# Splitting the first load of a between two DMA queues in a fused matmul, gelu, matmul kernel

## The chip, the core and the metric

The kernel runs on one core of one Trainium2 chip. The core has five engines that run beside each other, each through its own list of instructions: TensorE (PE in the profile, with its weight loads as PEld), VectorE (DVE), ScalarE (ACT), GpSimd (POOL) and SyncE (SP). Sixteen DMA engines move data between the chip's main memory and the core's memory of 128 partitions. The metric is the device time of one execution in microseconds (us); less is better. The time before is the median of three runs.

## The reference

```python
m, k, n, p = 1024, 1024, 2048, 1024     # a: m x k, b: k x n, c: n x p, all float32

def reference(a, b, c):
    h = np.matmul(a, b)
    h = 0.5 * h * (1 + np.tanh(np.sqrt(2 / np.pi) * (h + 0.044715 * h ** 3)))
    return np.matmul(h, c).astype(np.float32)
```

Two matrix products with the tanh form of gelu between them.

## The kernel before

The order of instructions on each engine is written out by hand; each engine runs its list from first to last and waits where an operand is not there yet.

The first product needs a transposed, with k on the partitions. So a's rows are cast to bf16 (`ab`), turned by TensorE with an identity matrix into PSUM (`pt`, L145) and copied by VectorE into `aT` (L146). b is needed with k on the partitions as it is, and only cast to bf16 (`b1`, `b2`). The result of a group of matmuls goes through gelu on ScalarE into `hT`, which the second product, with c, reads. The first columns of the first product are plain matmuls (`mm1`, L114); the rest of it and the whole second product go by a scheme of seven products of quarter matrices (`Seven`, L212), with the sums on VectorE and ScalarE. The output is stored by SP.

The stretch that matters here is the start. `a_part(h, q)` is half h of a's rows (512 rows, as four groups of 128) and quarter q of its columns (256), which is 512 KB. SP's queue issues five loads in float32, in this order:

- L75: `a_part(0, 0)` into `sta[:, 0, 0]`, 512 KB;
- L76: the first two k blocks of b's first 512 columns into `stb[:, 0:2]`, 512 KB;
- L77: `a_part(1, 0)` into `sta[:, 1, 0]`, 512 KB;
- L78: `a_part(0, 1)` into `sta[:, 0, 1]`, 512 KB;
- L79: the third k block of b into `stb[:, 2]`, 256 KB.

All other loads are issued by GpSimd, which casts them to bf16 on the way (L86 to L104: the rest of a into `abq`, of b, then c). GpSimd first copies one element of the first load's tile into `gate` (L81), so that its loads come after that landing.

ScalarE begins with one tiny gelu (L82), before which the activation table is loaded; its next work is a cast of b (L108). TensorE first runs matmuls on a constant (`stir`, L125), and then, in this order: the transposes of `a_part(0, 0)`, six matmuls with k blocks 0 and 1, the transposes of `a_part(1, 0)`, five matmuls, the transposes of `a_part(0, 1)`, and so on. VectorE casts all of `sta[:, 0, 0]` in one instruction (L110, by `cast_a(0, 0, nc.vector)`), copies the first transposes, casts a part of b, copies the second transposes, and shares the cast of `sta[:, 1, 0]` with ScalarE.

Of the kernel before, what the change touches and what calls it, by code (L numbers as in the profile page):

```python
# [19 lines left out]
def kernel(ctx, tc, a, b, c, out):  # L20
    nc = tc.nc
# [18 lines left out]
    def slot(tag, shape, dt, name):  # L40
        return big.tile(shape, dt, name=name, tag=tag)
# [24 lines left out]
    sta = slot("x1", [128, 2, 2, 4, 256], F32, "sta")  # L66
    abq = slot("x3", [128, 4, 2, 4, 256], BF16, "abq")

    def a_part(h, q):
        return av[:, 4 * h:4 * h + 4, ds(q * 256, 256)]  # L70

    def b_part(q):
        return bv[:, 2 * q:2 * q + 2, 0:H]

    nc.sync.dma_start(out=sta[:, 0, 0], in_=a_part(0, 0))  # L75
    nc.sync.dma_start(out=stb[:, 0:2], in_=b_part(0))  # L76
    nc.sync.dma_start(out=sta[:, 1, 0], in_=a_part(1, 0))  # L77
    nc.sync.dma_start(out=sta[:, 0, 1], in_=a_part(0, 1))  # L78
# [20 lines left out]
    for n in range(2):  # L99
        for k in range(0, KT, 4):  # L100
            nc.gpsimd.dma_start(out=b2[:, k:k + 4, ts(n, H)],
                                in_=bv[:, k:k + 4, ds(1024 + n * H, H)])
# [385 lines left out]
```

## Time and profile before

| What | us |
|---|---|
| median of three runs | 117.6 (117.41 to 117.97) |
| span of the profiled execution, first to last instruction | 115.7 |
| TensorE busy in it | 111.1 (96%) |
| VectorE busy | 90.0 (78%) |
| ScalarE busy | 51.4 (44%) |
| GpSimd busy | 17.2 (15%) |

For the profiled execution the page gives its span; the time of the runs holds what lies around the span as well. The granted TensorE clock was 1.000 of full speed. The DMA engines are mostly busy in the first 50 us, with loads, and in the last fifth, with stores. The five loads of SP's queue stand in the profile's rows as `sta<-in_a_dram` and `stb<-in_b_dram`; from issue to landing the three into `sta` took 3.6, 6.1 and 7.0 us, and the two into `stb` 5.3 and 7.1 us.

A row of the timeline gives start, duration, engine, line, operation, what it writes and reads, and in brackets how long the engine was idle before it and what ended that. A row "SPq" or a "DMA_DIRECT2D" is the issuing of a transfer, not the transfer. The chain of waits follows the work that ended last back to the start: each piece is what the next one was released by.

### The profile page before, as it was taken

The page shows a single profiled execution, that of the slowest core. Times are in us where ns is not written, and L with a number is a line of the kernel's source. Part 1 is how long each engine was busy: PE and PEld are TensorE (multiplying, and loading weights), DVE is VectorE, ACT ScalarE, POOL GpSimd, SP SyncE. Part 2 cuts the span into 40 slices and gives each one's busy share as a digit, 9 for nine tenths or more (in the row PEclk, how much of TensorE's full clock was granted, in tenths as well). Part 3 has the DMA queues.
Part 4 walks back from the last instruction along what each step waited for, and adds up shares of the span by engine and source line. Part 5 has one row for each costly group of instructions (what it writes and reads, how often), then busy time and mean ns, then how long its engine had stood idle before and what let it go on. Part 6 is the DMA issues. An engine that isn't in the chain of part 4 may idle for free.

```text
span 115.7 us, 1461 instructions
## 1 busy us (share of the span) xinstructions
PE 111.1 (96%) x542; PEld 77.1 (67%) x542; DVE 90.0 (78%) x107; ACT 51.4 (44%) x86; POOL 17.2 (15%) x29
## 2 busy tenths in 40 slices
PE   7989999999999999999999999999999999999980
PEld 6645555546776447888885444688888888888860
DVE  0347748789999998935699999999999986954770
ACT  5053000999259997166698429500124982000000
POOL 2497755223322000000000000000000000000000
PEclk9999999999999999999999999999999999999999
DMA  2999999999999999998000000060000002014993
GB/s 69 295 381 229 200 199 205 204 208 205 206 211 209 212 213 209 212 210 168 8 0 0 6 0 0 38 235 0 0 0 0 0 4 91 1 73 176 370 363 106
DMA packets 13414, 15.94 MB, mean 138 GB/s; under 512 B 736, under 2 KB 9312, under 8 KB 13408
## 3 DMA queue, kind: packets, MB, share of 16 engines
q0 software_dynamic: 8672, 9.31, 47.6%
q1 hardware_dynamic: 4736, 6.56, 15.8%
q8 instruction: 4, 0.07, 0.3%
q14 instruction: 2, 0.02, 0.0%
HBM read 20.97 MB, written 4.19 MB: 218 GB/s over the span
## 4 chain that ended last, share of the span: by engine, by line
PE 90%; DMA 5%; SPq 1%; DVE 1%; issue 0%
PE ps L212 76%; PE ps L114 11%; DMA sta<-in_a_dram 5%; PE pt L145 3%; SPq L76 0%; DVE ab L110 0%; SPq L75 0%; DVE ot L375 0%
## 5 line engine op out<-in xcount | busy, mean ns | idle before, releaser
L212 PE MATMUL ps<-x,s 128*128 128x512 f32 x128 | 29.6, 391 | 0.0
L212 PEld LDWEIGHTS ps<-x,s 128*128 128x128 f32 x128 | 24.0, 188 | 5.1
L212 PE MATMUL ps<-x,x 128*128 128x512 f32 x96 | 22.9, 394 | 0.0
L212 PEld LDWEIGHTS ps<-x,x 128*128 128x128 f32 x96 | 18.0, 188 | 3.9
L114 PE MATMUL ps<-aT,b 128*128 128x512 bf16 x64 | 16.1, 379 | 0.2 <-DVE b L110 0.2
L298 ACT ACTIVATE v<-ps 128x512 f32<-128x512 f32 x10 | 6.0, 599 | 19.1 <-PE ps L212 19.1
L212 PE MATMUL ps<-c_sb,hT 128*128 128x512 bf16 (+1 forms) x72 | 14.2, 356 | 0.0
L212 PE MATMUL ps<-x 128*128 128x512 f32 x56 | 13.2, 392 | 0.0
L212 PEld LDWEIGHTS ps<-x 128*128 128x128 f32 x56 | 10.2, 188 | 2.6 <-ACT u L298 0.4
L118 ACT ACTIVATE hT<-ps 128x512 bf16<-128x512 f32 x14 | 7.3, 595 | 9.7 <-PE ps L114 9.7
L212 PEld LDWEIGHTS <-hT 128*128 128x128 bf16 x72 | 6.9, 98 | 7.0 <-issue 0.5
L118 ACT ACTIVATE hT<-ot 128x512 bf16<-128x512 f32 x18 | 10.4, 624 | 2.0 <-DVE ot L303 2.0
L212 PE MATMUL ps<-aT,b 128*128 128x512 bf16 x48 | 10.7, 379 | 0.0
L146 DVE COPY aT<-pt 128x512 bf16<-128x512 bf16 x16 | 6.7, 423 | 5.1 <-PE pt L145 5.1
L303 DVE TENSOR_TENSOR ot<-ps,u 128x512 f32<-128x512 f32 x10 | 6.7, 690 | 5.1 <-ACT u L298 5.1
L303 DVE TENSOR_TENSOR ot<-ps,v 128x512 f32<-128x512 f32 x10 | 6.7, 688 | 4.8 <-DMA out_dram<-ot 3.8
L170 DVE TENSOR_TENSOR x<-c_sb 128x1024 fp32r<-128x1024 bf16 x8 | 9.3, 1226 | 0.0
L114 PEld LDWEIGHTS <-b 128*128 128x128 bf16 x64 | 5.7, 98 | 4.5 <-DVE b L110 0.3
L212 PEld LDWEIGHTS <-b 128*128 128x128 bf16 x48 | 4.6, 98 | 5.7 <-issue 0.3
L104 POOL DMA_DIRECT2D c_sb<-in_c_dram x8 | 5.6, 702 | 13.1 <-DMA b<-in_b_dram 12.4
L170 DVE TENSOR_TENSOR x<-b 128x1024 fp32r<-128x1024 bf16 (+1 forms) x4 | 7.0, 1752 | 0.6 <-issue 0.6
L298 ACT ACTIVATE u<-ps 128x512 f32<-128x512 f32 x10 | 5.9, 598 | 3.4 <-PE ps L212 3.2
(44 smaller groups left out, 111.3 us busy)
## 6 DMA issues: line engine op xcount, KB each, us to landing
c_sb<-in_c_dram POOLq DMA_DIRECT2D x8, 512.0 KB, 20.0
out_dram<-ot SPq DMA_DIRECT2D x13, 256.0 KB, 2.1
b<-in_b_dram POOLq DMA_DIRECT2D x6, 512.0 KB, 15.3
sta<-in_a_dram SPq DMA_DIRECT2D x3, 512.0 KB, 6.1
abq<-in_a_dram POOLq DMA_DIRECT2D x5, 256.0 KB, 7.9
out_dram<-ot SPq DMA_DIRECT2D x6, 128.0 KB, 2.0
stb<-in_b_dram SPq DMA_DIRECT2D x1, 512.0 KB, 5.3
b<-in_b_dram POOLq DMA_DIRECT2D x2, 256.0 KB, 8.2
```

Of the source, the lines that this page charges most:

```text
L104: nc.gpsimd.dma_start(out=c_sb[:, t:t + 2], in_=cv[:, t:t + 2])
L114: nc.tensor.matmul(p, b1[:, k, ts(t, 128)], aT[:, h, k], start=(k == 0), stop=(k == KT - 1))
L118: nc.scalar.activation(hT[h][:, t], p, AF.Gelu_apprx_tanh)
L145: nc.tensor.transpose(pt[:, n, ts(m, 128)], ab[:, m, ts(n, 128)], ident)
L146: nc.vector.tensor_copy(aT[:, h, 2 * q + n], pt[:, n])
L170: nc.vector.tensor_tensor(out=dst[:, r], in0=x[:, r], in1=y[:, r], op=op)
L212: nc.tensor.matmul(p[:, ds(c0, w)], l[:, k, ts(j, 128)], r[:, k, ds(c0, w)], start=(start and k == 0), stop=(k == self.kt - 1), skip_group ...
L298: nc.scalar.activation(st, p, AF.Copy)
L303: nc.vector.tensor_tensor(out=ot, in0=p, in1=st, op=ADD)
```

## The change

The first of SP's loads is cut in two by groups of rows. The groups 0 and 1 of `a_part(0, 0)` (rows 0 to 255) stay on SP's queue, and the groups 2 and 3 (rows 256 to 511) are issued by ScalarE, ahead of its tiny gelu. Everything else is the same, the instructions that read `sta[:, 0, 0]` included; these now depend on two transfers where they read both parts.

```diff
@@ -72,7 +72,8 @@
     def b_part(q):
         return bv[:, 2 * q:2 * q + 2, 0:H]
 
-    nc.sync.dma_start(out=sta[:, 0, 0], in_=a_part(0, 0))
+    nc.scalar.dma_start(out=sta[:, 0, 0, 2:4], in_=a_part(0, 0)[:, 2:4])
+    nc.sync.dma_start(out=sta[:, 0, 0, 0:2], in_=a_part(0, 0)[:, 0:2])
     nc.sync.dma_start(out=stb[:, 0:2], in_=b_part(0))
     nc.sync.dma_start(out=sta[:, 1, 0], in_=a_part(1, 0))
     nc.sync.dma_start(out=sta[:, 0, 1], in_=a_part(0, 1))
```

## The prediction

> **What bounds the kernel now.** I read the chain that ended last, then that chain in order of time, then the instructions of the first 20 us, then busy time and traffic by stretch. The chain by engine, from the page:
>
> ```profile
> PE 90%; DMA 5%; SPq 1%; DVE 1%; issue 0%
> ```
>
> TensorE is the path for nine tenths of the span; of the rest one load is the largest piece. In order of time (start us, us, what):
>
> ```profile
> 0.74 0.44 SPq L75
> 1.18 0.05 issue
> 1.24 0.50 SPq L76
> ...
> 1.78 6.10 DMA sta<-in_a_dram
> ...
> 7.90 0.44 DVE ab L110
> 8.34 0.05 issue
> 8.38 0.62 PE pt L145 x8
> ...
> 24.46 87.96 PE ps L212 x400
> ```
>
> From 8.38 us on the path is TensorE without a break. What sets 8.38 is the landing, at 1.78 + 6.10 = 7.88 us, of the third load on SP's queue, rows 512 to 1023 of a (L77), not of the load that is changed. So the change can only act through what it does to that landing, through delaying something that has slack now, or outside the span. The instructions around it (start us, us, engine, line, then in brackets the idle time before it):
>
> ```profile
> 0.74 1.28 ACT L82 ACT_TABLE_LOAD   x1 [0.74 <-PEq L472]
> ...
> 4.40 0.69 DVE L110 CAST ab<-sta 128x1024 bf16<-128x1024 f32 x1 [4.40 <-DMA sta<-in_a_dram]
> ...
> 5.08 0.87 POOL L86 DMA_DIRECT2D abq<-in_a_dram  x1
> ...
> 5.58 0.42 DVE L146 COPY aT<-pt 128x512 bf16<-128x512 bf16 x1 [0.49 <-PE pt L145]
> ...
> 6.54 0.94 ACT L108 ACTIVATE b<-stb 128x256 bf16<-128x256 f32 x2 [4.30 <-DMA stb<-in_b_dram]
> 6.54 0.36 DVE L110 CAST b<-stb 128x128 bf16<-128x128 f32 x2 [0.53 <-DMA stb<-in_b_dram]
> ...
> 6.83 1.47 PE L114 MATMUL ps<-aT,b 128*128 128x512 bf16 x6 [0.15 <-DVE b L110]
> ...
> 15.88 0.26 PEld L145 LDWEIGHTS <-abq 128*128 128x128 bf16 x4 [0.28 <-DMA abq<-in_a_dram]
> ```
>
> The first load of a lands just before 4.40. After its cast, transposes and first copy, VectorE stands idle 0.53 us until b lands at 6.54. That 0.53 us is the first load's slack: earlier by itself gains nothing, later by less costs nothing. Then the traffic by stretch (window in us, its length, busy time of each engine, clock, busy share of the DMA engines, and last GB/s):
>
> ```profile
> 1.60:2.00 0.40, 0.40 (x2) 0.31 (x2) 0.00 (x0) 0.40 (x1) 0.00 (x0) 1.00 0.07 26
> 2.00:2.40 0.40, 0.40 (x2) 0.31 (x2) 0.00 (x0) 0.23 (x2) 0.00 (x0) 1.00 0.54 138
> 2.40:2.80 0.40, 0.40 (x3) 0.31 (x2) 0.00 (x0) 0.00 (x0) 0.00 (x0) 1.00 0.91 259
> 2.80:3.60 0.80, 0.80 (x4) 0.62 (x3) 0.00 (x0) 0.00 (x0) 0.00 (x0) 1.00 1.07 364
> ...
> 4.00:5.60 1.60, 1.53 (x10) 1.03 (x9) 0.71 (x2) 0.00 (x0) 1.17 (x2) 1.00 0.91 260
> 5.60:9.00 3.40, 2.92 (x23) 1.66 (x23) 1.71 (x6) 1.56 (x3) 3.40 (x6) 1.00 1.08 380
> ```
>
> All five SP loads are issued by 2.83 + 0.55 = 3.38 us, yet the last lands near 9.93 (2.83 + 7.1 of its tile's view). So the stream is not short of issues: it climbs from nothing to 364 GB/s in one us, sags to 260 in the first b load, and runs at 380 after that.
>
> **The change, part by part.**
> *SP's issue.* One issue of 512 KB becomes one of 256 KB. The five SP issues take 0.44, 0.50, 0.46, 0.51 and 0.55 us, the smallest load the longest, so size does not set them: SP's later issues stay where they are. 0.
>
> *ACT's issue.* One DMA issue, 0.44 to 0.55 us by SP's rows, now ahead of the table load (1.28 us) and the small activation (0.20 us) on ScalarE. Covered by ScalarE's 4.30 us of idleness before 6.54; 0. Without that cover it would be 0.5 us. The same DMA issue is not moved past any SP or POOL issue.
>
> *The stream's start.* The bytes up to the end of L77's load are the same, so L77 lands earlier only if the stream runs better. What the climb loses against 380 GB/s: bytes start at about 1.84 us (finer slices), so 0.16 x 380 - 0.40 x 26 = 50 KB, then 0.40 x (380 - 138) = 97, 0.40 x (380 - 259) = 48, 0.80 x (380 - 364) = 13; together 208 KB, or 208 / 380 = 0.55 us. Two queues that each climb as this one did, added and cut at 380, would have by 2.80 us 20 + 110 + 152 = 282 KB in place of 10 + 55 + 104 = 169, and gain the 13 after it: 126 KB, 0.33 us. If one generator feeds both queues, nothing is gained: 0. If the whole climb went, 0.55. I take 0.3, the two climbs added, since in 2.00 to 2.40 the DMA engines are busy only 0.54 and so have room for a second supply.
>
> *Where the 0.3 us goes.* b, L77, L78 and L79 stand behind it on SP's queue and land as much earlier; VectorE's and ScalarE's casts wait for just these landings. The next thing late would be POOL's stream: TensorE's transposes at 15.93 waited until 15.88 for one of its loads, while TensorE's own work ran to 16.09 on the chain: 0.2 us of slack. POOL's first issue follows the gate copy, which waits for the first load, and POOL's bytes start to move about 9.0 us, as SP's run dry, so the stream should come forward too. If it doesn't, the gain ends at 0.2.
>
> *Second waits.* The first cast waits for two landings (the gate's one element lies in ScalarE's half). By the chain's "issue" pieces a wait costs 0.02 to 0.07 us, inside the 0.53 us of slack: 0.
>
> *Outside the span.* The page gives the span, 115.7 us, alone; the median of the runs is 117.6, so 1.9 us lie around it. ScalarE's hardware queue is not used before; setting it up or closing it is shown by no row. Between 0 and 0.8 us, the longest of SP's closing waits for stores; I take 0, since these waits are for bytes and this queue has been empty for 100 us by then, and keep the 0.8 in the range.
>
> Sum: 117.6 - 0.3 = 117.3 us, a span of 115.4.
>
> One rule speaks against this. The Trainium skill, "DMA: Bandwidth & Descriptors", section "Issuing engines are not separate DMA queues", says that DMAs started by different engines run on the same 16 DMA engines and interleave, and that several issuers save only issue time. By it the sum would be 117.6. This trace shows no second hardware queue at work, so it can neither confirm nor deny it.
>
> **The rivals.**
> *The sag fills too (faster).* If the second queue's reads also overlap the first b load's, part of the stretch 4.00 to 5.60 comes back: 1.60 x (380 - 260) = 192 KB, 0.50 us, on top of 0.3: 116.8. For it: the DMA engines are busy 0.91 at 260 GB/s, so single packets take longer there, as if they waited for memory. Against: ScalarE's half should be in before 4.00, and POOL's slack of 0.2 would then have to move as well.
>
> *ScalarE's half comes late (slower).* Place: ScalarE's queue. If the table load goes first, as it stands first now, the issue comes at 0.74 + 1.28 = 2.02 us and its bytes start 1.1 us later (1.84 - 0.74), at 3.1. SP's half is in by then and b's rows share the engines. 262 KB at a half to a third of some 300 GB/s take 1.75 to 2.6 us, and the last landings came about 0.5 us after the last bytes: the half lands between 5.3 and 6.1. The point from which it decides is 4.40 + 0.53 = 4.93; beyond that VectorE's copy, casts of b and TensorE's first matmuls go back by 0.4 to 1.2 us, and the matmuls stand before the transposes at 8.38. With 0.8: 118.4. For it: the load is ScalarE's first instruction now, at the same 0.74 as SP's first issue. Against: the issue stands ahead of that activation in the program, and the load bears the activation's line.
>
> *ScalarE's queue is starved (slower still).* POOL's first load was issued at 5.08 and no byte of it moved until 9.0, when SP's ran out: the queue view of 4.40 to 9.00 lists SP's queue alone. If ScalarE's half fares so, it lands with SP's last, about 9.9, some 5.5 us late, 5.0 beyond the slack: 122.6. Against: POOL's is a software queue, ScalarE's a hardware one issued together with SP's.
> That wait differs from "Queues, rings and completion order" of the same page of the skill, by which each DMA engine goes round its queues packet by packet; by that rule this rival is worth nothing.
>
> *A closing cost for the second queue:* 117.3 + 0.8 = 118.1. *Nothing at all,* one generator feeding both: 117.6.
>
> **How the numbers follow.** The forecast 0.36, its own range 117.0 to 117.6; the sag filled 0.27; the late half 0.20; starved 0.05; closing cost 0.08; nothing 0.04. A measurement of this kernel tells 0.5%, about 0.6 us, from no change. Faster: 0.27 and 0.04 of the forecast, where all of the climb goes, 0.31. Same: 0.32 of the forecast and 0.04, 0.36. Slower: 0.20 + 0.05 + 0.08 = 0.33. Cases of both signs hold over half, so the range goes from 116.7 (the sag filled, less 0.1 of scatter) to 118.6 (the late half, plus 0.2); starvation and the late half's worst are left out.
>
> **What would show it.** Right: ScalarE's first row an issue near 0.74; more than 138 GB/s in 2.00 to 2.40; the first cast before 4.40; b's casts near 6.2, the cast at 7.90 near 7.6, transposes at 8.1. Wrong: an issue after the table load; a first cast after 4.9; the same climb; a shorter span with the same time around it lost; POOL's stream still starting at 9.0, so that the wait at 15.88 grows.

## The result, and the profile after

The changed kernel takes 117.95 us (median of 22 runs) against 117.56 us before, a ratio of 1.003 with a 95% interval of 1.0019 to 1.0041: slower by 0.39 us by the medians and by 0.35 us by the ratio, where 0.3 us faster was forecast. The profiled execution has a span of 116.5 us against 115.7 us.

The chain of waits of the changed kernel in order of time (start us, us, what), its middle left out:

```profile
0.74 0.44 SPq L76
...
1.75 6.29 DMA sta<-in_a_dram
...
8.54 0.62 PE pt L146 x8
...
24.80 87.98 PE ps L213 x400
112.79 0.02 issue
112.81 0.42 DVE ot L376
```

The same last piece in the chain before:

```profile
112.44 0.42 DVE ot L375
```

The shape of the path is unchanged. Its start came 0.16 us later (8.54 against 8.38), TensorE's long stretch 0.34 us later, and the last addition 0.37 us later. This lateness is within what single executions differ by: six profiles with the changed loads (this one and five of the runs below) have the long stretch begin at 24.41 to 24.94 us, three with the loads as before at 24.46 to 24.81 us. But the span is 0.8 us longer. From the start of the last addition to the end of the span there are 115.67 - 112.44 = 3.23 us before and 116.47 - 112.81 = 3.66 us after (the ends to the hundredth, from the trace): 0.43 us were lost behind the last computation, where the change touches nothing.

Of the start, in the timeline (start us, us, engine, line, idle time before):

```profile
0.74 0.47 ACTq L75 DMA_DIRECT2D sta<-in_a_dram  x1
...
1.24 1.28 ACT L83 ACT_TABLE_LOAD   x1 [1.24 <-PEq L473]
...
4.59 0.69 DVE L111 CAST ab<-sta 128x1024 bf16<-128x1024 f32 x1 [4.59 <-DMA sta<-in_a_dram]
...
6.63 0.36 DVE L111 CAST b<-stb 128x128 bf16<-128x128 f32 x2 [0.35 <-DMA stb<-in_b_dram]
...
16.26 0.23 PEld L146 LDWEIGHTS <-abq 128*128 128x128 bf16 x4 [0.43 <-DMA abq<-in_a_dram]
```

ScalarE issued its half at 0.74 us, as SP did, yet the first load as a whole landed at 4.57 and not 4.38. VectorE's 0.53 us of slack before b's cast shrank to 0.35 us, so this lateness was covered. TensorE's wait for one of GpSimd's loads, 0.28 us before, is 0.43 us in the last row; it put 0.12 us on the path here, but was 0.22 and 0.24 us in two later profiles of the same loads. The traffic by stretch (window, its length, busy times, clock, DMA share, GB/s):

```profile
2.00:2.40 0.40, 0.40 (x2) 0.31 (x2) 0.00 (x0) 0.40 (x1) 0.00 (x0) 1.00 0.82 166
2.40:2.80 0.40, 0.40 (x2) 0.31 (x2) 0.00 (x0) 0.33 (x2) 0.00 (x0) 1.00 0.89 282
2.80:3.60 0.80, 0.80 (x4) 0.62 (x3) 0.00 (x0) 0.00 (x0) 0.00 (x0) 1.00 1.03 316
...
4.00:5.60 1.60, 1.60 (x8) 0.84 (x7) 0.69 (x1) 0.00 (x0) 0.98 (x2) 1.00 0.96 269
```

In 2.00 to 2.80 us this execution has 166 and 282 GB/s, the one before 138 and 259. That is no more than scatter: two later profiles with the loads as before have 146 and 310, and 192 and 323. The sag at 4.00 to 5.60 is still there.

At the end, the view of what SP waited for (engine, line, what: us in total, times, longest) differs. Before:

```profile
SPq L483 <- DMA out_dram<-ot: 1.1, 2, 0.8
```

After:

```profile
SPq L484 <- DMA out_dram<-ot: 1.5, 1, 1.5
```

Before, SP waited for stores twice, at most 0.8 us; after, once, 1.5 us. The trace's rows of SP, from its last store on, show why (ns from the span's start, duration, operation, semaphores; the first of a pair of waits is the completion of a hardware transfer from the second row on). Before, the last store signals semaphore 118:

```
112897 332 DMA_DIRECT2D     semaphore=118
113274  28 EVENT_SEMAPHORE  S[115] S[114]
113344  28 EVENT_SEMAPHORE  S[102] S[113]
113405  28 EVENT_SEMAPHORE  S[103] S[112]
...
113934  27 EVENT_SEMAPHORE  S[117] S[105]
114794  28 EVENT_SEMAPHORE  S[118] S[100]
114859   7 DRAIN
```

After, it signals semaphore 100:

```
113265 332 DMA_DIRECT2D     semaphore=100
113643  28 EVENT_SEMAPHORE  S[116] S[115]
115169  28 EVENT_SEMAPHORE  S[100] S[114]
115230  28 EVENT_SEMAPHORE  S[102] S[113]
...
115536  28 EVENT_SEMAPHORE  S[117] S[106]
115598  28 EVENT_SEMAPHORE  S[118] S[103]
115663   7 DRAIN
```

The hardware transfers of SP and ScalarE share eight completion semaphores, handed out in turn, and SP's closing list, the waits behind its last issue, checks the eight in that same order, one row about every 0.061 us. Before, 24 transfers make three full turns: the last store has the eighth semaphore, and the other rows of the list pass while it is under way. After there are 25: the last store has the first one. SP stands there until it lands, and then walks the seven other rows, 115.598 - 115.169 = 0.43 us, though the stores behind those had all landed by then, the latest 0.86 us before the last one.

### The profile page after: what moved, and what is told of

Read it like the earlier page. It is cut to its first block, busy times and chain, and to the rows that moved or that the text cites. A ratio compares the mean times of both kernels' runs of the same rounds, so it can differ in the third digit from the quotient of the medians.

```text
span 116.5 us, 1463 instructions
## 1 busy us (share of the span) xinstructions
PE 111.6 (96%) x542; PEld 77.3 (66%) x542; DVE 89.9 (77%) x107; ACT 51.4 (44%) x86; POOL 17.3 (15%) x29
## 4 chain that ended last, share of the span: by engine, by line
PE 90%; DMA 5%; SPq 1%; DVE 1%; issue 0%
PE ps L213 76%; PE ps L115 11%; DMA sta<-in_a_dram 5%; PE pt L146 3%; SPq L77 0%; DVE ab L111 0%; SPq L76 0%; DVE ot L376 0%
```

## The experiments

Five theories were on the table. Theory 1: bytes of a second queue between SP's make one DMA engine fall behind (a load lands in sixteen parts; in the profiled execution the sixteenth part of L77's load, L78 after, landed 0.38 us after the fifteenth, before 0.10). Theory 2: the cut itself costs. Theory 3: a second queue costs as such. Theory 4: GpSimd's gate opens later. Theory 5, formed after the first four runs, whose profiles showed the same 0.4 us at the end: the number of transfers decides which of the eight semaphores the last store gets. All ratios are against the kernel before on the same chip, with 95% intervals.

**Both halves on SP's queue.**

```diff
-    nc.sync.dma_start(out=sta[:, 0, 0], in_=a_part(0, 0))
+    nc.sync.dma_start(out=sta[:, 0, 0, 0:2], in_=a_part(0, 0)[:, 0:2])
+    nc.sync.dma_start(out=sta[:, 0, 0, 2:4], in_=a_part(0, 0)[:, 2:4])
```

> Both halves of the first load on SP's queue, none on ScalarE's. Theory 1, the second queue makes one DMA engine fall behind (last landing of L77's load 0.4 us after the fifteenth, in place of 0.1): no second queue, so the spread is as before (0.1) and the time is that of before, ratio 1.000 within 0.002. Theory 2, the cut itself costs (two transfers, two completions, SP's later issues 0.5 us later): the time is that of the changed kernel, 1.003.

Measured: 121.05 us, 1.0277 (1.0235 to 1.032). Neither theory: far slower than the changed kernel. It is taken up again below.

**A load of 512 bytes on ScalarE's queue, nothing cut** (into a tile `tiny` made for it).

```diff
+    nc.scalar.dma_start(out=tiny, in_=av[:, 0, 0:1])
     nc.sync.dma_start(out=sta[:, 0, 0], in_=a_part(0, 0))
```

> The kernel before, with one load of 512 bytes more, issued on ScalarE's queue at the start and read by nobody. Theory 1, bytes of a second queue between those of SP's on the DMA engines cost: 128 elements of 4 bytes are too little, 1.000 within 0.002. Theory 3, the second queue costs as such, however little it carries: 1.003.

Measured: 118.22 us, 1.0059 (1.0038 to 1.0079). One transfer that nobody reads costs as much as the change or more. This looked like theory 3, but the kernel also has 25 transfers; with 0.0036 taken off for the end, 0.002 is left for the start. In its profile the load that set the path, L77's before, landed at 8.20 us in place of 7.88; whether the tiny load does that every time was not followed up.

**The changed kernel with the gate on SP's half.**

```diff
-    nc.gpsimd.tensor_copy(gate, sta[:, 0, 0, 3, 0:1])
+    nc.gpsimd.tensor_copy(gate, sta[:, 0, 0, 1, 0:1])
```

> The changed kernel, but GpSimd's gate copy reads an element of SP's half (landed at 4.27 us) in place of ScalarE's (4.57). Theory 4, POOL's stream is late because the gate opens 0.2 us later: POOL's issues come 0.3 us earlier, the wait at 16.26 goes, and the ratio falls from 1.003 to 1.001. Theory 1: POOL's bytes moved at 8.79 us anyway, before they did at 9.01, so the gate is not it: 1.003 as the changed kernel.

Measured: 118.03 us, 1.0032 (1.0014 to 1.0051). Theory 4 falls. Theory 1 falls with it: in this profile L78's load landed at 7.85 us, its last part 0.11 us behind the fifteenth, and TensorE's long stretch began at 24.47 us, all as before, and still the kernel was 0.3% slower. The part that fell behind was the scatter of one execution.

**ScalarE's issue behind its activation.**

```diff
-    nc.scalar.dma_start(out=sta[:, 0, 0, 2:4], in_=a_part(0, 0)[:, 2:4])
     nc.sync.dma_start(out=sta[:, 0, 0, 0:2], in_=a_part(0, 0)[:, 0:2])
 ...
     nc.scalar.activation(g, warm[:, 0:1], AF.Gelu_apprx_tanh)
+    nc.scalar.dma_start(out=sta[:, 0, 0, 2:4], in_=a_part(0, 0)[:, 2:4])
```

The gate copy goes behind it too.

> The changed kernel with ScalarE's half issued behind the table load and the tiny gelu, near 2.24 us. By the slack of 0.53 us the half lands between 5.3 and 6.1 and the time is 0.4 to 1.2 us over before, ratio 1.003 to 1.010. Theory 1: more of that half runs beside b's load, so the spread of the landings stays at 0.4 or grows. If the issue time doesn't matter, 1.003.

Measured: 118.05 us, 1.0039 (1.0025 to 1.0053). The issue was not late at all. ScalarE's rows:

```profile
0.74 1.28 ACT L81 ACT_TABLE_LOAD   x1 [0.74 <-PEq L473]
0.80 0.46 ACTq L82 DMA_DIRECT2D sta<-in_a_dram  x1
2.03 0.20 ACT L81 ACTIVATE g<-const-float32-0.0 128x1 f32<-128x1 f32 x1
```

The issue stands third in ScalarE's program, behind the table load and the activation, and ran at 0.80 us, beside the table load and 1.2 us ahead of the activation. How ScalarE comes to issue it that early, no view shows. So the experiment did not delay the half, and the rival of the late half could not have come about by the table load.

**The changed kernel with 24 transfers.**

```diff
-        n = 2 if (i, l) == (0, 0) and j else 1
+        n = 2 if (i, l) == (0, 0) and j > 1 else 1
```

> The changed kernel, with two stores of 128 KB in the middle of the second product made one, so that SP and ScalarE issue 24 hardware transfers in all, as the kernel before does, and not 25. Theory 5, the count shifts which completion semaphore the last store uses, and so how many of SP's closing waits (0.061 us each) come after its landing: two as before, not nine, 7 x 0.061 = 0.43 us back, ratio 1.000 within 0.002. Theory 1 or 4, the loads at the start are late: 1.003 as the changed kernel.

Measured: 117.46 us, 0.9989 (0.9977 to 1.0). The loss is gone. (The two and nine of the expectation count SP's two drains behind the list.) In its profile, the chain's end and SP's wait:

```profile
112.50 0.42 DVE ot L376
```

```profile
SPq L484 <- DMA out_dram<-ot: 1.0, 2, 0.8
```

The last store has semaphore 118 again, the wait for it is 0.8 us again, and the span is 115.7 us.

**The kernel before with 25.** The same line, the other way:

```diff
-        n = 2 if (i, l) == (0, 0) and j else 1
+        n = 2 if (i, l) == (0, 0) else 1
```

> The kernel before, no load changed and no second queue, but one store of 256 KB in the middle of the second product cut in two: 25 hardware transfers. Theory 5: the last store gets the semaphore that is checked first, seven more waits come after its landing, 0.43 us, ratio 1.0036. Theory 1, 2 or 3 (second queue, cut load): 1.000 within 0.002.

Measured: 117.94 us, 1.0041 (1.0028 to 1.0054). No load is touched and no second queue is used, and the whole loss is there. SP's wait in its profile:

```profile
SPq L483 <- DMA out_dram<-ot: 1.5, 1, 1.5
```

This and the run ahead of it settle the cause: the loss follows the count, not the loads.

**The kernel before with 28**, by `n = 2 if (i, l) == (0, 0) or (i, l) == (1, 1) and j < 3 else 1`.

> The same with four stores cut in two: 28 hardware transfers, the last store's semaphore fourth of eight, four more waits after its landing. Theory 5: 4 x 0.061 = 0.24 us, ratio 1.002, less than with 25. If each added transfer costs by itself, four times that of 25.

Measured: 117.78 us, 1.0017 (0.9993 to 1.0041). The size is as expected, but the interval tells it neither from nothing nor from the 1.0041 of 25. The trace shows the mechanism: the last store's row passed at 115.141 us and the last row of the list at 115.383, four rows and 0.24 us later.

**The changed kernel with 24, gate on SP's half.** Both edits from above.

> The changed kernel with 24 hardware transfers and the gate on SP's half. Theory 5: 1.000, and if the cut at the start gains anything once POOL is let go 0.3 us earlier, below 0.999. Theory 4 beside theory 5: 0.001 below the same kernel with the gate on ScalarE's half.

Measured: 117.48 us, 0.9995 (0.9985 to 1.0005). Releasing GpSimd earlier gains nothing on top that these intervals show.

**Both halves on SP's queue, 24 transfers.**

> Both halves of the first load on SP's queue, and 24 hardware transfers. Theory 5: only the 0.43 us of the closing waits come back from 1.0277, so 1.024; the rest is the stretch of b's first load, which again runs at about 140 GB/s in 4.00 to 5.60 us. If the slow stretch was chance, 1.000.

Measured: 120.67 us, 1.0261 (1.0225 to 1.0297). The count gives back 0.0016 where 0.0036 was expected; the two intervals leave room for that. The slow stretch came again:

```profile
2.00:2.40 0.40, 0.40 (x2) 0.31 (x2) 0.00 (x0) 0.22 (x2) 0.00 (x0) 1.00 0.77 253
2.40:2.80 0.40, 0.40 (x2) 0.31 (x2) 0.00 (x0) 0.00 (x0) 0.00 (x0) 1.00 1.03 361
...
3.60:4.00 0.40, 0.40 (x3) 0.31 (x2) 0.00 (x0) 0.00 (x0) 0.00 (x0) 1.00 0.32 100
4.00:5.60 1.60, 0.98 (x7) 0.55 (x6) 0.69 (x1) 0.00 (x0) 0.97 (x2) 1.00 0.56 117
```

The climb (253 and 361 GB/s, and 225 and 384 in the first run of this cut) is steeper than before, and the sag (117 GB/s, and 139) the deepest of all runs. b's first load landed at 8.89 us, 2.4 us later than before; its sixteen parts came in between 5.99 and 8.89 us, before between 5.95 and 6.51.

**b's first load cut as well, 24 transfers** (no store is cut, `n = 1`; a's first load is cut on SP's queue as above).

```diff
-    nc.sync.dma_start(out=stb[:, 0:2], in_=b_part(0))
+    nc.sync.dma_start(out=stb[:, 0], in_=bv[:, 0, 0:H])
+    nc.sync.dma_start(out=stb[:, 1], in_=bv[:, 1, 0:H])
```

> As the last but one, and b's first load cut in two as well, one k block each, like SP's last load, whose rows came at about 400 GB/s in 8.6 to 9.0 us. If two rows of b per partition in one transfer make the slow stretch, it goes: over 300 GB/s in 4.00 to 5.60 us and 0.998 to 1.000. If the engines' common start makes it, it stays at about 140 GB/s and the ratio at 1.02.

Measured: 120.18 us, 1.0222 (1.0198 to 1.0247), at 172 GB/s in 4.00 to 5.60. Two rows of b in one transfer are not the cause, or not all of it. That the engines' common start is, the other reading, was not shown by this.

**The changed kernel with 32, by cut stores.** `n = 2 if (i, l) in ((0, 0), (1, 1)) or (i, l) == (0, 1) and j < 2 else 1`.

> The changed kernel with seven more stores cut in two: 32 hardware transfers, four rounds of eight semaphores, so the last store's is checked last again. Theory 5, the place in the list decides: 1.000 within 0.002, in spite of eight more transfers than before. If the number of transfers costs, more than the 1.004 of 25.

Measured: 118.19 us, 1.0055 (1.0038 to 1.0071): a miss. The edit put stores on the path. Its chain near the end:

```profile
106.07 0.33 SPq L430
106.45 0.43 SPq L430
106.93 0.46 SPq L430
107.43 2.10 DMA out_dram<-ot
109.65 0.70 DVE ot L435
```

VectorE waited for buffers whose stores had come later, one issue after another. The run's time says nothing on the semaphores. Its trace does: the last store has semaphore 118, and its row, at 115.463 us, is the last of the list.

**The changed kernel with 32, by small loads in a gap of SP's** (again into a tile `tiny`).

```diff
+        if (i, l, j) == (0, 0, 2):
+            for t in range(7):
+                nc.sync.dma_start(out=tiny[:, t:t + 1], in_=av[:, 0, t:t + 1])
```

> The changed kernel with seven loads of 512 bytes more on SP's queue, issued in the middle of the second product, where SP waits some 18 us for its next store: 32 hardware transfers, and the stores near the end as they were. Theory 5, the place of the last store's semaphore decides: with 32 it is checked last again, and the ratio is 0.998 to 1.001, although this kernel does all that the changed one does and more. If the number of transfers or the second queue costs, 1.003 or more.

Measured: 117.81 us, 1.0003 (0.9986 to 1.002). Seven transfers more than the changed kernel, and the loss is gone: the last store has semaphore 118 and its row, at 115.241 us, is again the last of the list. SP's wait:

```profile
SPq L488 <- DMA out_dram<-ot: 1.0, 3, 0.5
```

So it is the place in the turn of eight and not the number.

All fourteen profiles agree on the end. From the landing of the last store to the end of the span there are 0.88 to 0.89 us in the seven with 24 or 32 transfers, 1.13 us in the one with 28, and 1.31 to 1.32 us in the six with 25, whichever loads or stores were touched.

## Why the prediction was wrong

**What bounds the kernel: right.** The path runs through the landings of SP's loads and then TensorE to the end, before and after.

**SP's and ScalarE's issues at no cost: right.** SP's later issues begin at 1.24, 1.75, 2.25 and 2.80 us (before 1.24, 1.78, 2.29, 2.83), and ScalarE's 0.47 us lie under its idle time. Second waits too: no row shows one on the path.

**"I take 0.3, the two climbs added": mis-sized.** With the end put right, the change is worth 0.9989 (0.9977 to 1.0): 0.13 us, at most 0.27, and perhaps nothing. ScalarE's bytes did not climb beside SP's: in six profiles of the changed loads they began at 2.22 to 2.64 us, SP's at 1.81 to 1.83, though both were issued within 0.01 us. Summing the packets of the trace that had begun by a given time, before there were 573 KB by 4.00 us and 990 KB by 5.60 us. The same six profiles had 604 to 666 KB and 1009 to 1037 KB: 19 to 47 KB ahead at 5.60, which is 0.05 to 0.12 us at 380 GB/s. The scatter is larger: two more profiles with the loads of before had 590 and 684 KB, and 985 and 1048 KB. The landing of the third load, which set the path in the profile before, shows no gain either: 7.77 to 8.03 us in the six, 7.87 to 7.92 us in the three.

**Under "Outside the span", "I take 0, since these waits are for bytes and this queue has been empty for 100 us by then": this step failed.** It set the sign. The cost is in the span, in SP's closing list; and that list is not only waits for bytes, since each row takes 0.061 us even when its transfer has long landed. What matters is how many rows stand behind the one that comes last. The forecast priced the added transfer by its issue alone and never asked which semaphore the last store would get. 0.43 - 0.13 = 0.30 us is within what was measured, 0.35 (0.22 to 0.48), and so is 0.43 alone. The rival "a closing cost for the second queue" had the place and, with 118.1 us, nearly the time, at a chance of 0.08; its reason was wrong, since no second queue is needed.

**The rivals.** The sag filled: no, 269 GB/s against 260 in that stretch, and 225 to 258 in the other five profiles of the changed loads. The late half and the starved queue: no; the half landed at 4.57 us, under the 4.93 from which lateness counts. It does share the engines: ScalarE's packets ran from 2.34 to 4.27 us, beside SP's. As for the rule of the Trainium skill, "DMA: Bandwidth & Descriptors", section "Issuing engines are not separate DMA queues", that several issuers save only issue time: the start alone came out at 117.56 x 0.9989 = 117.43, between the sum by that rule, 117.6, and mine, 117.3, and its interval reaches the rule's. The packets agree that the two hardware queues interleave.

**What stays open.** Why a first load cut on one queue makes b's stretch fall to 117 to 172 GB/s and the kernel 2.2 to 2.8% slower is not known; that it does was measured in three kernels. Whether the changed loads gain anything at all at the start is open too.

## What to carry to other kernels

Adding a single transfer moved the time by some tenths of a us at the very end, through the place that the last store's completion has in SP's closing list; before an effect of that size is put down to the edit, compare the time from the last computation to the span's end, and repeat the edit with the count of transfers put back. Aim for a count that gives the last store the last place in the turn (here a multiple of eight). A gain at the start of a stream has to be checked at the landing that is waited for, since a slower stretch behind it can take it back, as with both halves on SP's queue; and in several profiles, since one alone scattered here by as much as the gain that was forecast.

## What the runs showed that was not expected

- A DMA issue in ScalarE's program did not wait for the table load and the activation ahead of it: it ran at 0.80 us while the load lasted from 0.74 to 2.02 us.
- Two hardware queues issued within 0.01 us began to move bytes 0.4 to 0.8 us apart, SP's first, in six profiles. With the load of 512 bytes it was the other way: ScalarE's first packet began at 1.77 us, SP's at 1.98 us.
- With the first 512 KB as one load from SP, the stretch of the next load ran at 227 to 260 GB/s in three profiles; with the same bytes as two loads from SP, at 139 and 117 GB/s.
- Each row of SP's closing list behind the last store's cost 0.061 us: 0.43 us for seven, 0.24 us for four.
